# One input projection of a gated encoder block, moved from a two-stage product to a seven-product scheme done token-major beside the norm

## The chip, the core and the metric

The kernel runs on one core of a Trainium2 chip. A core has a matrix engine (TensorE, in the profile PE for its products and PEld for the loading of its stationary operands), a vector engine (VectorE, DVE), a scalar engine (ScalarE, ACT), a general engine (GpSimd, POOL) and a queue engine (SyncE, SP) that mostly issues transfers. Every engine works through its own instructions strictly in their order and waits where one of them needs something that is not there yet. Transfers that SP, ACT or POOL issue are moved by 16 DMA engines, which all of them share. On-chip memory is SBUF; PE writes into PSUM banks.

The metric is the time of one execution on the device in microseconds. Three runs of the kernel before gave a median of 924.56 us, from 924.12 to 924.88.

## What is computed

The reference is one layer of a gated encoder with 1024 tokens of width 1024. Cut to what matters here:

```python
h = rmsnorm(x, norm_g[l])
proj = h @ w_in[l]
q, k, v, za, u, vs, zs, gm = jnp.split(proj, IN_SPLITS, axis=-1)
...
sgo = chunked_spatial_gating(jax.nn.gelu(u, approximate=False),
                             jax.nn.gelu(vs, approximate=False),
                             sg_w[l], sg_b[l], sg_ln_g[l], sg_ln_b[l])
```

`chunked_spatial_gating` takes a layer norm over the 1024 channels of gelu(vs), and mixes blocks of 128 tokens. This case is about `vs` alone: a product of 1024 tokens by 1024 inputs by 1024 outputs, in single precision.

## The kernel before

Every product in this kernel is taken in three passes: an operand is split into a high part of the type fp32r (a cast on ACT) and the residual (a subtraction on DVE), and high by high, high by low and low by high are added in PSUM. One instruction multiplies a 128x128 stationary block with 512 columns. All products but that of `vs` use a seven-product scheme (Strassen's, in a form with four sums of weights and four sums of activations): both operands are cut into quarters, and seven quarter products stand in for eight. Its activation forms are called b11, t1, t2, b21, t3, b22 and t4 and lie in the slots `T_b11h`, `T_b11l` and so on (h is the high part, l the residual); `gemm_pair` walks through them (line 341 is its matmul).

`vs` comes first, and its layout is token-major: the tokens are the stationary operand, 512 output channels are the moving one. Here the eight products are all made, in two stages.

- **Stage 1, lines 599 to 621.** Tile t is 128 tokens, t from 0 to 7. `normed_tile` scales the rows of a tile (`scale_of`: a square with a sum on ACT, a few one-column instructions, then two multiplications of 512 columns at line 545), turns them with eight transposes on PE (line 551) and makes the high part (line 554, ACT) and the residual (line 555, DVE); a plain copy of each half goes to a raw slot (line 558, ACT). `vs_gemm` then takes the first 512 output channels of one tile: 8 blocks of inputs by 3 passes, 24 matmuls (line 596). Four weight tiles of 512 KB each are loaded into `T_t3h` and `T_t4h` (line 571) and split into `T_t1` and `T_t2` by `split_vs`. The program runs three tiles of the norm ahead of the products.
- **Stage 2, lines 680 to 705.** The last 512 output channels, for all eight tiles at once: eight PSUM banks, four weight tiles split through the rotating tiles `wh` and `wl` (line 156), and for each of them 8 tiles by 2 blocks by 3 passes (line 565). In between, `make_forms` builds t1, t2, t3 and t4 for the rest of the kernel from the raw slots, the gelu of the first half is taken (line 637), and `part_of_early` issues one transfer on POOL's queue after every second group (line 296): these add up weight sums of much later products in DRAM, and each of them waits for a matmul.
- Then the sums of rows of the mixing weights (line 712), a few small loads, and the first `gemm_pair`.

The instructions of each engine are put in an order of their own when the program is built, by a list scheduler that works on the program order and the tiles' dependencies; a load of the small constants can therefore stand between two loads of x. Tiles of one tag share a fixed number of buffers: x tiles and raw weight tiles share the three buffers of `wr`, so the load of x tile t can start once tile t-3 has been turned.

Two more facts of queues and buffers. A transfer that adds (`accum_op=ALU.add`) can only be issued by POOL, and POOL's queue is in order too. And the `junk` tile, into which line 531 writes the squares that nobody reads, is a `wl` buffer here, while the tile `wT` is only used for the mixing weights (loaded at line 681, cleared in part at line 682 on DVE).

Of the kernel before, what the change touches and what calls it, by code (L numbers as in the profile page):

```python
# [24 lines left out]
F32 = mybir.dt.float32  # L25
F32R = mybir.dt.float32r
# [4 lines left out]
P = 128  # L31
# [21 lines left out]
def hybrid_tile(  # L53
# [117 lines left out]
    def slot(name, shape=(P, 4, HALF), dt=F32R):  # L171

        return mtile(list(shape), dt, "T_" + name, 1)
# [317 lines left out]
    junk = mtile([P, D], F32, "wl", 3)  # L491
# [11 lines left out]
    g_in = [bank("o") for half in range(2)]  # L503
    for half in range(2):
# [4 lines left out]

    b12 = [  # L510
        [v[:].rearrange("p (a k c) -> p a k c", a=2, k=4)[:, i] for i in range(2)]
        for v in (mtile([P, D], F32R, "s", 2) for _ in range(2))
    ]
    b12 = [(hi, mtile([P, 4, P], F32R, "x", 5)[:]) for two in b12 for hi in two]
    f = {n: slot(at, dt=F32) for n, at in (("f11", "t3l"), ("f21", "t4l"))}
# [4 lines left out]
    def quarter_of(t, j):  # L520

        if t >= 4 and j == 0:
            return b12[t - 4]
        return [v[:, :, tokens(t)] for v in hb[("b11", "b21", "b22")[j if t < 4 else 2]]]

    casts = []

# [9 lines left out]
    def normed_tile(t, scale=None):  # L537
        xt, r = scale or scale_of(t)
        if t == 4:
            hb.update(new_b(("b22",)))  # L540
            f.update((n, slot(at, dt=F32)) for n, at in (("f12", "t4h"), ("f22", "t3h")))
        turned = []
        for j in range(2):
            cs = half_of(j)
            nc.vector.scalar_tensor_tensor(
                xt[:, cs], xt[:, cs], r[:], g_in[j][:], op0=ALU.mult, op1=ALU.mult
            )
            pt = bank("tp")
            for i in range(4):
                k = j * 4 + i  # L550
                nc.tensor.transpose(pt[:, i * P : (i + 1) * P], xt[:, k * P : (k + 1) * P], ident[:])
            p3 = pt[:].rearrange("p (k c) -> p k c", k=4)
            hi, lo = quarter_of(t, j)
            casts.append(nc.scalar.copy(hi, p3))
            nc.vector.tensor_sub(lo, p3, hi.bitcast(F32))
            turned.append((f[f"f{j + 1}{t // 4 + 1}"][:, :, tokens(t)], p3))
            if t:
                nc.scalar.copy(*turned.pop())
        return turned

    def vs_step(acc, t, k, wh, wl):

        hi, lo = (v[:, k % 4, :] for v in quarter_of(t, k // 4))
        for n, (lt, rt) in enumerate(((hi, wh), (hi, wl), (lo, wh))):
            mm = nc.tensor.matmul(acc, lt, rt, start=k == 0 and n == 0, stop=k == KC - 1 and n == 2)  # L565
        return mm

    vs_w = []

    def load_vs(c):  # L570
        nc.sync.dma_start(vs_raw[c // 2][:, c % 2, :], w[W_VS + c])

    def split_vs(c):

        raw = vs_raw[c // 2][:, c % 2, :].rearrange("p (k n) -> p k n", k=2)
        hi, lo = (v[c // 2][:, 2 * (c % 2) : 2 * (c % 2) + 2, :] for v in vs_split)
        if c:
            split(hi, lo, raw)
        else:

            for k in range(2):
                nc.scalar.copy(hi[:, k, :], raw[:, k, :])
                (nc.gpsimd if k else nc.vector).tensor_tensor(
                    lo[:, k, :], raw[:, k, :], hi[:, k, :].bitcast(F32), op=ALU.subtract
                )
        vs_w.extend((hi[:, k, :], lo[:, k, :]) for k in range(2))

    def vs_gemm(t):
        acc = bank("mm")
        for c in range(4):  # L590
            for n in range(3):
                for k in (2 * c, 2 * c + 1):
                    hi, lo = (v[:, k % 4, :] for v in quarter_of(t, k // 4))
                    wh, wl = vs_w[k]
                    lt, rt = ((hi, wh), (hi, wl), (lo, wh))[n]
                    nc.tensor.matmul(acc[:], lt, rt, start=k == 0 and n == 0, stop=k == KC - 1 and n == 2)  # L596
        nc.scalar.copy(xh[:, t, 0:HALF], acc[:])

    unsplit = normed_tile(0)
    keep_busy(0)  # L600
    vs_raw = [slot(n, (P, 2, D), F32) for n in ("t3h", "t4h")]
    vs_split = [[slot(n + e) for n in ("t1", "t2")] for e in "hl"]
# [8 lines left out]
    x_in[2] = load_x(2)  # L611
    for c in (2, 3):
        split_vs(c)
    for dst, src in unsplit:
        nc.scalar.copy(dst, src)
    normed_tile(1, second)
    normed_tile(2)
    for t in range(NT):
        vs_gemm(t)
        if t + 3 < NT:  # L620
            normed_tile(t + 3)


    def vs_weights(c):
        raw = raw_tile()
        nc.sync.dma_start(raw[:], w[W_VS + 4 + c])
        hi = mtile([P, D], F32R, "wh", 3)
        lo = mtile([P, D], F32R, "wl", 3)
        split(hi[:], lo[:], raw[:])
        return hi, lo  # L630
# [4 lines left out]
    def gelu_of(t):  # L635
        two = xh[:, t : t + 2, 0:HALF]
        after(nc.scalar.activation(two, two, AF.Gelu), casts[-1])
        for i in range(2):
            statistics(t + i, 0)

    def form(name, src, c):
        hi, lo = hb[name]
        cs = slice(c, c + 2)
        split(hi[:, cs, :], lo[:, cs, :], src, name == "t2")

    def make_forms():
        f11, f12, f21, f22 = (f[n] for n in ("f11", "f12", "f21", "f22"))
        hb.update(new_b(("t1",)))
        for c in range(0, 4, 2):
            cs = slice(c, c + 2)  # L650
            nc.vector.tensor_sub(f11[:, cs, :], f11[:, cs, :], f12[:, cs, :])
            form("t1", f11[:, cs, :], c)
            yield
        hb.update(new_b(("t2",)))
        for c in range(0, 4, 2):
            cs = slice(c, c + 2)
            nc.vector.tensor_add(f11[:, cs, :], f22[:, cs, :], f11[:, cs, :])
            form("t2", f11[:, cs, :], c)
            yield
        for c in range(0, 4, 2):  # L660
            cs = slice(c, c + 2)
            nc.vector.tensor_sub(f12[:, cs, :], f22[:, cs, :], f12[:, cs, :])
            yield
        last = []
        for c in range(0, 4, 2):
            cs = slice(c, c + 2)
            v = mtile([P, 2, HALF], F32, "s", 2)
            nc.vector.tensor_sub(v[:], f11[:, cs, :], f21[:, cs, :])
            last.append(v)
            yield  # L670
        hb.update(new_b(("t3",)))
        for c in range(0, 4, 2):
            form("t3", f12[:, c : c + 2, :], c)
            yield
        hb.update(new_b(("t4",)))
        for c in range(0, 4, 2):
            form("t4", last[c // 2][:], c)
            yield
# [6 lines left out]
    accs = [bank(tag) for tag in ("mm", "mm", "o", "o", "sc", "sc", "tp", "tp")]  # L685
    aside = [lambda t=t: gelu_of(t) for t in range(0, NT, 2)]
    forms = make_forms()
    aside[1:1] = [lambda: next(forms, None)] * 2
    aside += [lambda: next(forms, None)] * 11
    weights = [vs_weights(0), vs_weights(1)]  # L690
    for c in range(4):
        if c + 2 < 4:
            weights.append(vs_weights(c + 2))
        for t in range(NT):
            wh, wl = weights[c]
# [4 lines left out]
            if c == 3:  # L700
                nc.scalar.activation(xh[:, t, HALF:D], accs[t][:], AF.Gelu)
            if aside and t % 2:
                aside.pop(0)()
    while aside:
        aside.pop(0)()

    row_sums = [bank("sc") for half in range(2)]
    wh, wl = mtile([P, D], F32R, "wh", 3), mtile([P, D], F32R, "wl", 3)
    split(wh[:], wl[:], mix_w[:].rearrange("p g i -> p (g i)"))
    for half in range(2):  # L710
        for n, part in enumerate((wh, wl)):
            nc.tensor.matmul(row_sums[half][:], ones[:], part[:, half_of(half)], start=n == 0, stop=n == 1)
    of_head = sinks.rearrange("(c e r) -> e c r", e=2, r=2)
# [8 lines left out]
    for _ in range(3):  # L722
        split_next()
# [1022 lines left out]
```

## Time and profile before

| | us |
|---|---|
| median of three runs | 924.56 |
| lowest and highest | 924.12, 924.88 |
| span of the profiled execution | 921.3 |
| PE busy in that span | 904.7 |
| DVE busy | 691.5 |
| ACT busy | 521.8 |
| POOL busy | 126.8 |

The span runs from the first instruction of the program to the end of the last one; the time of a run is taken around the whole execution and is some 3.3 us longer (924.56 - 921.3). Three kinds of view are used below. The waits tell which engine stood still for whom. The timeline lists instructions with their start and duration, both in us. The windows give, for a stretch of time, the busy us of each engine with the number of its instructions in brackets, then the granted clock of PE (1.00 is full), the mean busy share of the DMA engines and the rate that they moved. Matmuls overlap, so the duration of one (0.39 us for 512 columns) is not its cost; the distance from one start to the next is.

### The profile page before, as it was taken

Reading aid. Unit: us, or ns where it says so; the run is one execution under the profiler, and the core shown is the slowest. Engines: PE = TensorE matmul, PEld = TensorE weight load, DVE = VectorE, ACT = ScalarE, POOL = GpSimd, SP = SyncE. Lnnn points to the kernel's source line nnn. Section 1 sums busy time; section 2 is a strip of 40 time slices with the busy share of each in tenths; the row PEclk is TensorE's granted clock in tenths of the full one; section 3 lists DMA queues with packets and bytes.
Section 4 is the critical chain, followed back from the end, with each engine's and each line's share of the span. In section 5 each row is a group of like instructions: output and inputs, shape, how many; then the busy total and the mean of one; then the engine's idle time right before and its main releaser. Section 6 shows DMA issues by size and latency. Waiting matters only on the chain.

```text
span 921.3 us, 13177 instructions
## 1 busy us (share of the span) xinstructions
PE 904.7 (98%) x4332; PEld 752.7 (82%) x4332; DVE 691.5 (75%) x1241; ACT 521.8 (57%) x1046; POOL 126.8 (14%) x188
## 2 busy tenths in 40 slices
PE   8999999999999999999999999999998999999996
PEld 5888888888888788888888888888877887878885
DVE  6875776656687668887778888747798589579996
ACT  6862443334444366767766766755665385367443
POOL 0002122213011001211101111101100111110012
PEclk9999999999999999999999999999999999999998
DMA  6427678877788676776786799689869755998632
GB/s 240 138 91 215 207 197 184 161 158 234 230 290 267 229 200 182 169 202 184 197 240 222 248 220 253 174 313 349 294 219 341 240 201 151 272 307 303 206 115 114
DMA packets 128734, 201.71 MB, mean 219 GB/s; under 512 B 12345, under 2 KB 60729, under 8 KB 128666
## 3 DMA queue, kind: packets, MB, share of 16 engines
q1 hardware_dynamic: 109512, 148.17, 48.8%
q0 software_dynamic: 19008, 52.44, 23.8%
q8 instruction: 34, 0.56, 0.3%
q14 instruction: 34, 0.28, 0.1%
q10 hardware_dynamic: 146, 0.27, 0.1%
HBM read 144.07 MB, written 86.11 MB: 250 GB/s over the span
## 4 chain that ended last, share of the span: by engine, by line
PE 85%; DVE 8%; DMA 4%; issue 2%; ACT 1%; SPq 1%; DVEq 0%; ACTq 0%
PE ps_mm L341 34%; PE ps_o L341 25%; PE ps_mm L596 5%; PE ps_sc L1076 3%; PE ps_o L1161 2%; PE ps_tp L341 2%; PE ps_tp L1120 2%; PE ps_sc L341 2%; PE ps_tp L764 2%; DVE wl L156 1%; PE ps_tp L565 1%; PE ps_sc L565 1%; PE ps_o L565 1%; PE ps_mm L565 1%; DVE bq L185 1%
## 5 line engine op out<-in xcount | busy, mean ns | idle before, releaser
L155 ACT CAST wh<-s 128x1024 fp32r<-128x1024 f32 (+1 forms) x78 | 78.1, 1005 | 87.2 <-PE ps_mm L341 49.9
L156 DVE TENSOR_TENSOR wl<-wr,wh 128x1024 fp32r<-128x1024 f32 (+1 forms) x80 | 75.7, 948 | 49.1 <-ACT wh L155 48.3
L155 ACT CAST wh<-wr 128x1024 fp32r<-128x1024 f32 (+1 forms) x80 | 66.3, 830 | 71.6 <-PE ps_mm L341 34.3
L156 DVE TENSOR_TENSOR wl<-s,wh 128x1024 fp32r<-128x1024 f32 (+1 forms) x78 | 90.9, 1166 | 9.3 <-ACT wh L155 9.2
L341 PE MATMUL ps_o<-T_t1h,wh 128*128 128x512 f32 x148 | 58.9, 398 | 0.8 <-ACT wh L155 0.7
L341 PE MATMUL ps_o<-T_b22h,wh 128*128 128x512 f32 x148 | 58.2, 394 | 0.0
L341 PE MATMUL ps_o<-T_t1h,wl 128*128 128x512 f32 x148 | 57.9, 391 | 0.3 <-DVE wl L156 0.3
L341 PE MATMUL ps_o<-T_b22l,wh 128*128 128x512 f32 x148 | 57.9, 391 | 0.0
L341 PE MATMUL ps_o<-T_b22h,wl 128*128 128x512 f32 x148 | 57.8, 390 | 0.0
L341 PE MATMUL ps_o<-T_t1l,wh 128*128 128x512 f32 x148 | 57.6, 390 | 0.0
L341 PE MATMUL ps_mm<-T_b11h,wl 128*128 128x512 f32 x140 | 54.8, 392 | 2.9 <-DVE wl L156 2.9
L341 PE MATMUL ps_mm<-T_t4h,wh 128*128 128x512 f32 x140 | 55.3, 395 | 0.5 <-DVE x L376 0.5
L341 PE MATMUL ps_mm<-T_t3l,wh 128*128 128x512 f32 x140 | 54.6, 390 | 0.6 <-DVE T_t3l L156 0.6
L341 PE MATMUL ps_mm<-T_t2h,wl 128*128 128x512 f32 x140 | 55.0, 393 | 0.0
L341 PE MATMUL ps_mm<-T_t2l,wh 128*128 128x512 f32 x140 | 55.0, 393 | 0.0
L341 PE MATMUL ps_mm<-T_b11h,wh 128*128 128x512 f32 x140 | 54.9, 392 | 0.0
L341 PE MATMUL ps_mm<-T_t3h,wh 128*128 128x512 f32 x140 | 54.9, 392 | 0.0
L341 PE MATMUL ps_mm<-T_t2h,wh 128*128 128x512 f32 x140 | 54.7, 391 | 0.0
L341 PE MATMUL ps_mm<-T_t4h,wl 128*128 128x512 f32 x140 | 54.7, 391 | 0.0
L341 PE MATMUL ps_mm<-T_t3h,wl 128*128 128x512 f32 x140 | 54.7, 390 | 0.0
L341 PE MATMUL ps_mm<-T_b11l,wh 128*128 128x512 f32 x140 | 54.6, 390 | 0.0
L1089 ACT ACTIVATE pr<-ps_sc,sm 128x192 f32<-128x192 f32 (+2 forms) x128 | 50.9, 410 | 6.5 <-DVE sm L1085 5.5
(356 smaller groups left out, 2399.6 us busy)
## 6 DMA issues: line engine op xcount, KB each, us to landing
wr<-in_w_dram SPq DMA_DIRECT2D x86, 256.0 KB
sums<-in_w_dram POOLq DMA_DIRECT2D x20, 512.0 KB, 5.6
s<-sums SPq DMA_DIRECT2D x20, 512.0 KB
q_hl<-qhl SPq DMA_DIRECT2D x16, 512.0 KB
q<-q_hl SPq DMA_DIRECT2D x64, 128.0 KB
wr<-in_w_dram SPq DMA_DIRECT2D x14, 512.0 KB
y_dr<-x POOLq DMA_DIRECT2D x28, 256.0 KB, 6.6
g<-in_w_dram POOLq DMA_DIRECT2D x12, 512.0 KB, 7.2
```

The costliest lines, as they stand in the source:

```text
L155: nc.scalar.copy(hi, src)
L156: return nc.vector.tensor_sub(lo, src, hi.bitcast(F32))
L185: op(dst[:, i : i + 2, :], a[:, i : i + 2, :], c[:, i : i + 2, :])
L341: nc.tensor.matmul(acc, lt, rt, start=fresh and k == 0 and n == 0, stop=k == 3 and n == 2, skip_group_check=True,)
L565: mm = nc.tensor.matmul(acc, lt, rt, start=k == 0 and n == 0, stop=k == KC - 1 and n == 2)
L596: nc.tensor.matmul(acc[:], lt, rt, start=k == 0 and n == 0, stop=k == KC - 1 and n == 2)
L764: nc.tensor.matmul(pm[:, t * P : (t + 1) * P], xh[:, half * 4 + t, g * P : (g + 1) * P], bias[-1][1][:, g % 4, :], start=True, stop=True,)
L1076: nc.tensor.matmul(sc[:, i, k0:], q_of[:, c, i * P : (i + 1) * P], kt[:, f, k0:], start=f == 0, stop=f == 1,)
L1089: nc.scalar.activation(held_in[c, i], sc[:, i, lo:hi], AF.Exp, bias=nmax[:, c, i : i + 1], scale=-1.0, accum_out=sums[:, c, i : i + 1],)
L1120: nc.tensor.transpose(dst, pr[:, i, block * P : block * P + width], ident[:])
L1161: nc.tensor.matmul(po[:, cs], lt, rt, start=n == 0, stop=n == len(terms) - 1)
```

## The change

`vs` is taken by the seven-product scheme too, token-major. With j the half of the tokens (tiles 0 to 3, and 4 to 7) and i the half of the output channels, four quarters of the result lie in `xh` as `x_place(i, j, t)`.

- For tiles 0 to 3 `first_tile` makes the forms b11 and b21, and `first_product` multiplies them by the weight quarters a11 and a12 (24 matmuls a tile, as before, but into two banks that are then added on ACT and DVE).
- For tiles 4 to 7 `second_tile` makes t1 and b22, on DVE from PSUM and from the copies that `first_tile` left in `xh`. Two adding transfers per tile (256 KB each, SBUF to SBUF) finish what t3 and t4 need.
- `by_s1` multiplies t1 by the weight sum s1 = a21 + a22, `by_s4` multiplies b22 by s4 = a12 + a11 + s1 (12 matmuls each a tile). `late_product` then takes t2 by s2 = a11 + s1, t3 by s3 = a21 + a11 and t4 by a22, 48 matmuls each, into the four banks that hold the b11 products.
- The weight sums are made by adding transfers on POOL's queue straight into the SBUF slots that hold the raw quarters: eight of 512 KB for s1, s4 and s2 and two more for s3, whose slot is loaded again (`load_part("s3", ...)`) once s1 has been read by all the others.
- `junk` is now in the buffer `wT`; x tiles 0 to 3 are turned through the banks `sc`, the gain stays in the banks `tp` until ACT copies it into `xh`.
- The stage of the forms (`make_forms`), and the four raw slots that it read, are gone.

The diff, cut to its core:

```diff
-    junk = mtile([P, D], F32, "wl", 3)
+    junk = mtile([P, D], F32, "wT", 1, pool)
+    nf12 = [xtile() for _ in range(4)]
...
+    def add_on(dst, src):
+        nc.gpsimd.dma_start(dst, src, accum_op=ALU.add)
...
+    def first_tile(t, scale=None):
+        xt, r = scale or scale_of(t)
+        left = []
+        for j, name in enumerate(("b11", "b21")):
+            pt = turned_half(xt, r, j)
+            form_of(name, t, by_k(pt[:]))
+            if j:
+                left.append(lambda pt=pt: nc.scalar.mul(raw_b21(t), pt[:], -1.0))
+            else:
+                left.append(lambda pt=pt: nc.scalar.copy(raw_sum(t), pt[:]))
+            if t:
+                left.pop()()
+        return left
+
+    def second_tile(t):
+        xt, r = scale_of(t)
+        if t == 4:
+            hb.update(new_b(("t1", "b22")))
+            f22.append(slot("t4l", dt=F32))
+        pt = turned_half(xt, r, 0)
+        nc.vector.tensor_sub(raw_sum(t), raw_sum(t), pt[:])
+        nc.scalar.mul(nf12[t - 4][:], pt[:], -1.0)
+        form_of("t1", t, by_k(raw_sum(t)))
+        pt = turned_half(xt, r, 1)
+        form_of("b22", t, by_k(pt[:]))
+        nc.scalar.copy(f22[0][:, t - 4, :], pt[:])
+        nc.vector.tensor_add(raw_sum(t), raw_sum(t), pt[:])
+        add_on(nf12[t - 4][:], f22[0][:, t - 4, :])
+        add_on(raw_b21(t), raw_sum(t))
...
+    def first_product(t):
+        accs[t] = bank("mm" if t < 2 else "tp")
+        vs_product(accs[t], "b11", t, "a11", True)
+        m2 = bank("o")
+        vs_product(m2, "b21", t, "a12", True)
+        nc.scalar.copy(x_place(0, 0, t), m2[:])
+        nc.vector.tensor_add(x_place(0, 0, t), x_place(0, 0, t), accs[t][:])
+
+    def by_s1(t):
+        t5s[t] = bank("o" if t < 2 else "sc")
+        vs_product(t5s[t], "t1", t, "s1", True)
+        nc.scalar.mul(x_place(1, 1, t), t5s[t][:], -1.0)
+
+    def by_s4(t):
+        vs_product(t5s[t], "b22", t, "s4", False)
...
     for c in (2, 3):
         load_vs(c)
     x_in[2] = load_x(2)
+    load_part("s1", "t4h", 1, 0)
     for c in (2, 3):
         split_vs(c)
...
+    for c in range(2):
+        add_on(flat(two_k(raws["s1"], c)), w_vs(1, 1, c))
+    for c in range(2):
+        add_on(flat(two_k(raws["a12"], c)), w_vs(0, 0, c))
+    for c in range(2):
+        add_on(flat(two_k(raws["a12"], c)), flat(two_k(raws["s1"], c)))
+    raws["s4"] = raws["a12"]
+    first_tile(1, second)
...
+    first_tile(2)
+    first_product(0)
+    first_tile(3)
+    first_product(1)
+    second_tile(4)
+    s1_hl = slot("t2h"), slot("t2l")
+    for c in range(2):
+        hi, lo = (two_k(v, c) for v in s1_hl)
+        split(hi, lo, two_k(raws["s1"], c))
...
+    first_product(2)
+    second_tile(5)
+    for c in range(2):
+        add_on(flat(two_k(raws["a11"], c)), flat(two_k(raws["s1"], c)))
+    raws["s2"] = raws["a11"]
+    first_product(3)
+    for c in range(2):
+        split_w("s4", c)
+    second_tile(6)
+    by_s1(0)
+    by_s1(1)
+    load_part("s3", "t4h", 1, 0)
+    for c in range(2):
+        add_on(flat(two_k(raws["s3"], c)), w_vs(0, 0, c))
+    second_tile(7)
+    by_s4(0)
+    by_s4(1)
+    a22 = []
+    for c in range(2):
+        a22.append(raw_tile())
+        nc.sync.dma_start(a22[c][:], w_vs(1, 1, c))
+    by_s1(2)
+    by_s1(3)
...
-    accs = [bank(tag) for tag in ("mm", "mm", "o", "o", "sc", "sc", "tp", "tp")]
...
-            for k in range(2):
-                ks = half_of(k)
-                pace[0] = vs_step(accs[t][:], t, 2 * c + k, wh[:, ks], wl[:, ks])
-            part_of_early()
...
+    late_product(
+        "t2",
+        "s2",
+        to_x12,
+        [lambda: split_w("s3", 0), make_t3]
+        + [lambda t=t: part_of("t3", t) for t in range(4)]
+        + [lambda: gelu_of(0), lambda: gelu_of(2)],
+    )
...
+    split_w("a22", 1, a22[1][:])
+    begin_job()
+    late_product("t4", "a22", to_x21, [split_next, lambda: gelu_of(4, 1), lambda: gelu_of(6, 1)])
```

More of the change, by code (lines that the diff above doesn't have):

```diff
@@ L501, in hybrid_tile @@
     keep_busy(2)
-    g_in = [bank("o") for half in range(2)]
+    g_in = [bank("tp") for half in range(2)]
     for half in range(2):
@@ L585, in split_vs, with vs_product @@
                 )
[L586 to L590, printed above, removed]
+        keep_w(name, c % 2, hi, lo)
+    def vs_product(acc, name, t, weight, fresh, last=True, cs=(0, 1)):
+        bh, bl = hb[name]
+        for c in cs:
             for n in range(3):
                 for k in (2 * c, 2 * c + 1):
[L593 to L597, printed above, removed]
@@ L603, in hybrid_tile, with keep_t5 @@
+    def by_s4(t):
+        vs_product(t5s[t], "b22", t, "s4", False)
+    def keep_t5(t):
+        nc.scalar.copy(x_place(0, 1, t), t5s[t][:])
+    unsplit = first_tile(0)
+    for name, at in (("a11", "t3h"), ("a12", "t3l")):
+        raws[name] = slot(at, dt=F32)
     load_vs(0)
@@ L611, in hybrid_tile @@
     x_in[2] = load_x(2)
+    load_part("s1", "t4h", 1, 0)
     for c in (2, 3):
         split_vs(c)
[L614 to L630, printed above, removed]
+    for move in unsplit:
+        move()
@@ new lines, in hybrid_tile @@
+    for c in range(2):
[6 more added lines that the diff above has]
+    first_tile(1, second)
+    g_sb = xh[:, 6:8, HALF:D]
+    for half in range(2):
+        after(nc.scalar.copy(g_sb[:, half, :], g_in[half][:]), casts[-1])
+    g_of[:] = [g_sb[:, half, :] for half in range(2)]
@@ L632, in statistics @@
+    for t in range(4):
+        form_of("t2", t, by_k(raw_sum(t)), True)
+    by_s4(2)
+    by_s4(3)
+    split_w("s2", 1)
+    for t in range(4):
+        keep_t5(t)
     def statistics(t, half):
         nc.vector.bn_stats(stats[:, t, half, :], xh[:, t, half_of(half)])
[L635 to L678, printed above, removed]
@@ L680, in hybrid_tile, with gelu_of @@
+    def gelu_of(t, half=0):
+        two = xh[:, t : t + 2, half_of(half)]
+        after(nc.scalar.activation(two, two, AF.Gelu), last_cast)
+        if half == 0:
+            for i in range(2):
+                statistics(t + i, 0)
     mix_w = mtile([P, KC, P], F32, "wT", 1, pool)
@@ L721, in hybrid_tile @@
     nc.sync.dma_start(lb_sb[:], ln_b)
-    for _ in range(3):
+    for _ in range(2):
         split_next()
```

175 lines of the change are left out of this document (111 added, 64 removed).

## The prediction

> **What bounds the kernel now.** I read the page's busy shares and its chain first, then what PE waited for in the stretch of the change, then the windows of that stretch.
>
> ```profile
> span 921.3 us, 13177 instructions
> ...
> PE 904.7 (98%) x4332; PEld 752.7 (82%) x4332; DVE 691.5 (75%) x1241; ACT 521.8 (57%) x1046; POOL 126.8 (14%) x188
> ...
> PE 85%; DVE 8%; DMA 4%; issue 2%; ACT 1%; SPq 1%; DVEq 0%; ACTq 0%
> ```
>
> ```profile
> PE ps_sc L498 <- DVE T_b22l L494: 1.9, 1, 1.9
> PE ps_tp L551 <- issue: 0.5, 1, 0.5
> ```
>
> ```profile
> 0.00:10.00 10.00, 7.57 (x17) 3.91 (x17) 4.63 (x11) 5.58 (x9) 2.13 (x8) 1.00 0.81 282
> 10.00:20.00 10.00, 9.85 (x41) 7.32 (x41) 7.90 (x19) 8.47 (x16) 0.00 (x0) 1.00 0.64 221
> 20.00:30.00 10.00, 10.00 (x52) 7.91 (x52) 8.08 (x24) 8.16 (x18) 0.00 (x0) 1.00 0.46 155
> ...
> 50.00:60.00 10.00, 10.00 (x46) 8.29 (x45) 6.99 (x10) 4.42 (x6) 0.00 (x0) 1.00 0.15 52
> ```
>
> PE is the bound, of the whole and of this stretch: the two rows of waits are all that it waited for in the first 260 us. In stage 1 ACT and DVE are 80% busy and PE still never waits. So a matmul that is dropped is worth its pitch, as long as PE is fed as densely as now; and DMA engines that are half idle are what the new adding transfers will use. The pitch is read from the end of stage 2:
>
> ```profile
> 97.72 0.39 PE L565 MATMUL ps_o<-wl,T_b21h 128*128 128x512 f32 x1
> ...
> 105.43 0.39 PE L565 MATMUL ps_tp<-wh,T_b22l 128*128 128x512 f32 x1
> 105.66 0.39 PE L712 MATMUL ps_sc<-wh,ones 128*128 128x512 f32 x1
> ...
> 106.59 0.39 PE L341 MATMUL ps_mm<-T_b11h,wh 128*128 128x512 f32 x1
> ```
>
> 35 matmuls stand from 97.72 to 105.43, so the pitch is 7.71 / 34 = 0.227 us. The first `gemm_pair` starts at 106.59; all behind it is the same in both kernels, so what this start moves, the end moves.
>
> **The gain.** Before: 8 tiles by 2 halves by 24 matmuls, 384. After: 24 for tiles 0 to 3, and 12 each for s1, s4, s2, s3 and a22 over four tiles, 4 x (24 + 60) = 336. 48 x 0.227 = **10.9 us** off the path if nothing new stops PE.
>
> **The price of an adding transfer.** The trace has none into SBUF. The nearest are 512 KB adds into DRAM: the last three of the group below, issued one behind the other, ran alone in 540 to 546.
>
> ```profile
> L442 POOL DMA_DIRECT2D g<-in_w_dram x12: 515/536/1424, 459.9 to 537.7; - x12
> ...
> DMA to landing us min/median/max: 3.6/7.0/13.3
> ```
>
> ```profile
> 4.00:12.00 8.00, 7.48 (x18) 4.29 (x19) 5.50 (x13) 5.90 (x11) 1.40 (x1) 1.00 1.00 365
> 540.00:546.00 6.00, 6.00 (x35) 5.15 (x35) 5.20 (x13) 3.33 (x11) 0.82 (x1) 1.00 1.04 191
> ```
>
> Both windows have all 16 engines busy; loads move 365 GB/s, adds 191. So 524 kB cost 1.44 us of the engines as a load and 2.74 as an add. For an add into SBUF I take 2.74: the share of 1.04 says that the engines themselves were full, not that DRAM was awaited. Its bounds are 1.44 (as a load) and 3.7 (the slowest landed after 13.3, third in its row; less 2.3, which a load takes beyond its engine time, below: 11.0 / 3). The Trainium skill, "Collectives: The Full Stack", section "The bandwidth ceiling: the fold count and why AG ≠ RS ≠ AR", says that an add in a transfer is slow since it needs two source reads through one ring, wherever they lie; half of 365 is 183 GB/s, an estimate of 2.87 us per add, and with it the sum below would come out about 1 us later. The trace's 191 agrees, and no run here shows the SBUF side yet.
>
> **First stall: the first half of s1.** As the changed kernel is built, PE makes tiles 0 and 1 as before, and comes to tile 2 where it does now:
>
> ```profile
> 12.80 1.23 DVE L156 TENSOR_TENSOR T_t2l<-T_t4h,T_t2h 128x1024 fp32r<-128x1024 f32 x1 [0.79 <-ACT T_t2h L155]
> ...
> 14.46 1.22 DVE L156 TENSOR_TENSOR T_t2l<-T_t4h,T_t2h 128x1024 fp32r<-128x1024 f32 x1
> ...
> 18.04 0.33 SPq L487 DMA_DIRECT2D wr<-in_x_dram  x1
> ...
> 23.00 8.73 SPq L487 DMA_DIRECT2D wr<-in_x_dram  x3
> ...
> 24.39 0.41 PEld L596 LDWEIGHTS ps_mm<-T_t1h,T_b11h 128*128 128x128 f32 x2
> ```
>
> In ACT's queue the cast of s1's first half stands right before the b11 cast of tile 2, which tile 2's product needs, so ACT, and PE behind it, wait for the landing of that sum. On POOL's queue the sum is third: the two adds of a11 onto a12 come first, and wait until a12 has been split, 14.0 and 15.7 (ends of the first two rows). So it is issued at about 16.2 (0.5 us an issue). When does it land? By 10.0 the engines have moved 2.82 MB, 5.4 loads; nine are due now (x0 to x2, a11, a12, and the new a21), the last at 10 + 3.6 x 1.44 = 15.2. Beside the adds come x3, x4 (18.04), x5 (23.00) and a bias of half the size, 3.5 x 1.44 = 5.0; three adds are 8.2. Shared engines give 15.2 + 5.0 + 8.2 = 28.4, and about 1 until the semaphore: **29.5**.
>
> ```profile
> L155 ACT CAST wh<-wr 128x1024 fp32r<-128x1024 f32 x5 | 5.3, 1059 | 8.4 <-PE ps_tp L565 7.9 <-DMA wr<-in_w_dram 0.5
> ...
> L554 ACT CAST T_b11h<-ps_tp 128x512 fp32r<-128x512 f32 x4 | 2.4, 588 | 1.9 <-PE ps_tp L551 1.9
> ```
>
> With 1.06 and 0.59 for the two casts PE goes on at 31.1: it stood 31.1 - 24.4 = **6.7 us**. The residual of that b11 is behind s1's residual on DVE, another **0.4**.
>
> **Second stall: x tile 6.** The slot of a21 is loaded again for s3, and this load waits for all adds that read s1. SP's queue is in order, and behind it stand the loads of x6 and x7. s1's second half lands at 29.5 + 2.74 = 32.2; four adds (two onto a12, two onto a11) wait for the halves and run behind it, 11.0 more: 43.2. Then half of a21 and x6:
>
> ```profile
> 0.74 0.39 SPq L487 DMA_DIRECT2D wr<-in_x_dram  x1
> ...
> 4.43 1.06 ACT L531 ACTIVATE wl<-wr 128x1024 f32<-128x1024 f32 x1 [1.64 <-DMA wr<-in_x_dram]
> ```
>
> A load takes 4.43 - 0.74 = 3.7 to arrive; x6 is there at 43.2 + 0.4 + 1.44 + 3.7 = 48.7. On ACT its square (1.06) stands before the copy of the s1 product of tile 0 (0.59), and s4 of tile 0 may not add into that bank before the copy: 50.4. PE had 60 matmuls and 16 transposes from 31.5, 13.6 + 2.1 (half a tile's four take 0.52, below), so it is through at 47.2: **3.2 us**.
>
> ```profile
> 26.34 0.55 PEld L551 LDWEIGHTS ps_tp<-ident,wr 128*128 128x128 f32 x4
> ...
> 26.86 0.30 PEld L596 LDWEIGHTS ps_mm<-T_t1h,T_b11h 128*128 128x128 f32 x2
> ```
>
> **Third stall: the mixing weights.** Their load is now behind the last square, since `junk` took their buffer; before, it went out at 10.60 and was covered.
>
> ```profile
> 10.60 0.43 SPq L681 DMA_DIRECT2D wT<-in_sg_w_dram  x1
> ...
> 19.72 0.48 DVE L682 MEMSET wT<- 64x512 f32 x1 [0.16 <-DMA sink_sb<-in_sinks_dram]
> ```
>
> x7 comes two loads behind x6 with an add of s3 between, 48.7 + 2.9 + 2.7 = 54.3; its square ends at 55.4, and the load arrives at 59.1 alone or 61.8 with one add ahead of it. I take 61. On DVE the memset stands before the residuals of tile 6 and the scaling of tile 7: 0.48, then three of 0.69, some small ones and the scaling:
>
> ```profile
> L545 DVE SCALAR_TENSOR_TENSOR wr<-wr,st,ps_o 128x512 f32<-128x512 f32 x16 | 11.2, 745 | 0.2
> ...
> L555 DVE TENSOR_TENSOR T_b11l<-ps_tp,T_b11h 128x512 fp32r<-128x512 f32 x4 | 2.8, 690 | 2.5 <-ACT T_b11h L554 2.5
> ```
>
> So tile 7 is turned at about 64.4. PE has 36 matmuls and 16 transposes from 50.4 and is there at 60.7: **3.7 us**. The casts of tile 7 that the next product waits for add about **0.9**.
>
> **The clock.** Behind a wait of 1.4 us PE's granted clock was halved once in this trace:
>
> ```profile
> PE ps_sc L1076 <- ACT pr L1089: 1.4, 1, 1.4
> ```
>
> ```profile
> 325.50:329.00 3.50, 3.50 (x12) 2.71 (x11) 2.13 (x9) 2.97 (x14) 0.00 (x0) 0.51 0.90 207
> ```
>
> 3.5 us at half rate lose 1.7. Behind stalls 1 and 2 the next stall, set by transfers, absorbs that; behind the third nothing does: **1.7**.
>
> **What costs nothing.** The last part (t2, t3, t4) is 144 matmuls, 32.7 us of PE, over six splits of weights (1.06 ACT, 1.22 DVE), twelve forms (0.59, 0.69), some eight sums (0.69) and the statistics, about 25 us of DVE and 20 of ACT; without that cover each split would cost 2.3. Fifteen paced transfers stand where sixteen did. The loads of the first `gemm_pair` go out some 20 us later, still over 30 us ahead of use.
>
> **Sum.** 6.7 + 0.4 + 3.2 + 3.7 + 0.9 + 1.7 = 16.6, less 10.9: +5.7. The profiled execution is 921.3 and some 3.3 around it, 924.6, which is the median of the runs too. Forecast: **930.3 us**.
>
> **Rivals.**
> - *Adds into SBUF run like loads* (1.44). s1 lands at about 15.2 + 5.0 + 4.3 + 1 = 25.5, PE stands 2.7; the chain for x6 ends ten microseconds earlier, before PE needs it, and mixing weights too. 2.7, the small 0.4 and 0.9, and the clock's 1.7, now not absorbed, are 5.7 against 10.9: 924.6 - 5.2, **919.4**. For it: the sum is neither read from DRAM nor written to it. Against it: the full engines in 540 to 546. It wins from an add under 2.1 us on.
> - *Adds into SBUF are slower still* (3.7). Eight stand on the way to x6: 8 x 0.96 = 7.7 more, **938**. For it: 13.3 us, and loads of x in between; against it: the median of that group is 7.0.
> - *The clock stays low longer*: each of the three stalls followed by two half windows, 3.4 where 1.7 is counted and 1.5 of stall 2 not absorbed, **933.5**. The Trainium skill, "TensorE: Matmul & The Clock Gate", section "Part 1: The HAM clock gate", has the gate close after a window of about 3.4 us without work; by that rule stalls 1 and 3 alone would bring it, and the row above, after 1.4, goes further.
> - *The casts don't hold PE*: if s1's split came late enough, all 10.9 stay: **913.7**. Against it: the built order of ACT's queue.
>
> **How the numbers follow.** Forecast 0.57, adds like loads 0.15, slower adds 0.12, clock 0.11, no stall 0.05. 0.2% (1.8 us) is about what runs of this kernel tell from no change. Faster: 0.15 + 0.05 = 0.20; within: 0.05, from the near end of the forecast's own range (926 to 935); slower 0.75. The range holds all but the last rival: 919 to 939.
>
> **What would show it.** Right: PE idle some 6 us from about 24 with ACT waiting for a transfer into `T_t4h`, again near 47 behind x6 and near 61 behind DVE's memset of `wT`; s1's halves landing near 30; the first L341 at about 112. Wrong: an add of 512 KB into SBUF that lands within 4 us in a row of three, PE dense from 24 to 50, and an L341 before 106.

## The result, and the profile after

| | median us | runs, from to | ratio to the kernel before |
|---|---|---|---|
| before, beside it | 924.3 | 4, 922.8 to 924.9 | |
| changed | 938.7 | 4, 937.8 to 941.2 | 1.0166, 95% interval 1.0147 to 1.0185 |
| changed, run again (e5 below) | 941.2 | 5, 938.0 to 944.1 | 1.0184, 1.0165 to 1.0203 |

The change costs 14 to 17 us where 5.7 were forecast. The profiled execution of the changed kernel was the slowest of its four: 941.2 us for a span of 939.4, 2.5 above the median. Runs that list both have 1.8 us between span and time, so the profiled 921.3 us of before belong to a run about 1 us faster than the median. Of the 18.1 us between the two spans 3.5 are therefore such differences.

The page of the changed kernel, busy shares and chain:

```profile
span 939.4 us, 13191 instructions
...
PE 904.0 (96%) x4284; PEld 749.5 (80%) x4284; DVE 697.7 (74%) x1263; ACT 528.3 (56%) x1060; POOL 142.9 (15%) x206
...
PE 80%; DVE 8%; DMA 7%; issue 2%; ACT 1%; SPq 0%; DVEq 0%; ACTq 0%
```

PE makes 48 matmuls less and is busy just as long (904.0 us; before 904.7): some of them took longer. DMA holds 7% of the chain instead of 4%. What PE waited for, over the whole span (us in all, times, longest):

```profile
PE ps_tp L650 <- ACT T_b11h L557: 5.0, 1, 5.0
PE ps_sc L548 <- DVE wr L544: 4.3, 1, 4.3
PE ps_mm L341 <- DVE wl L156: 2.9, 2, 1.7
PE ps_mm L341 <- ACT x L366: 2.3, 1, 2.3
PE ps_o L650 <- ACT xh L674: 2.1, 2, 1.8
...
PE ps_tp L650 <- DVE T_b11l L558: 1.7, 1, 1.7
PE ps_sc L650 <- ACT x L581: 1.2, 1, 1.2
PE ps_tp L880 <- DVE xh L858: 1.1, 2, 0.8
PE ps_tp L880 <- DVE x L896: 0.9, 1, 0.9
```

The three stalls of the prediction are there: tile 2 (5.0 and 1.7), the bank behind x6's square (1.8), tile 7 (4.3 and 1.2). The 2.9 is in both kernels. The rows of L366, L858 and L896 are new, and they lie behind the start of the first `gemm_pair`, where nothing was forecast: a fourth stall. The timeline says what held ACT and DVE (start, duration, then the idle time before it and what ended it):

```profile
28.15 1.04 ACT L155 CAST T_t2h<-T_t4h 128x1024 fp32r<-128x1024 f32 x1 [6.56 <-DMA T_t4h<-in_w_dram]
29.10 0.58 ACT L557 CAST T_b11h<-ps_sc 128x512 fp32r<-128x512 f32 x1
...
31.55 0.20 DVE L834 TENSOR_SCALAR nsink_sb<-sink_sb 128x8 f32<-128x8 f32 x1 [9.77 <-DMA sink_sb<-in_sinks_dram]
...
51.15 1.06 ACT L536 ACTIVATE wT<-wr 128x1024 f32<-128x1024 f32 x1 [2.08 <-DMA wr<-in_x_dram]
...
64.83 0.48 DVE L768 MEMSET wT<- 64x512 f32 x1 [5.15 <-DMA wT<-in_sg_w_dram]
...
118.30 0.39 PE L341 MATMUL ps_mm<-T_b11h,wh 128*128 128x512 f32 x1
...
125.98 0.69 DVE L242 TENSOR_TENSOR s<-wr 128x512 f32<-128x512 f32 x1 [6.95 <-DMA wr<-in_w_dram]
```

Each wait in brackets ends with a transfer. Two were not in the prediction: `nsink` (L834), a negation of eight numbers per partition that stands on DVE ahead of tile 2's residuals and waits 9.8 us for a 2 KB transfer, and the weight sums of the second job (L242), 7.0 us. The first L341 starts at 118.30; before it was 106.59, so 11.7 us are lost ahead of it and 6.4 behind. Stretches of the span (length, busy us and count of PE, PEld, DVE, ACT, POOL, then granted clock, DMA share, GB/s):

```profile
24.90:28.35 3.45, 0.00 (x0) 0.00 (x0) 0.00 (x0) 0.20 (x1) 0.00 (x0) 1.00 1.00 176
28.35:38.58 10.23, 7.12 (x16) 5.14 (x17) 6.15 (x13) 5.58 (x10) 3.46 (x4) 0.50 1.04 239
38.58:41.00 2.42, 2.42 (x17) 2.04 (x16) 0.80 (x3) 1.33 (x4) 0.00 (x0) 1.00 1.09 217
62.90:65.89 2.99, 0.36 (x2) 0.00 (x0) 1.03 (x2) 0.00 (x0) 0.00 (x0) 1.00 1.07 296
65.89:76.13 10.24, 7.35 (x21) 5.68 (x22) 6.77 (x13) 5.01 (x7) 3.45 (x4) 0.50 0.81 164
...
100.00:110.00 10.00, 10.00 (x46) 8.26 (x45) 8.20 (x11) 5.07 (x5) 2.75 (x4) 1.00 0.98 247
110.00:120.00 10.00, 10.00 (x46) 8.29 (x45) 8.21 (x21) 4.35 (x6) 2.64 (x5) 1.00 0.95 262
```

Behind the first and the third stall the clock is halved for 10.2 us each time, not for 3.4; a start every 0.43 us instead of 0.227 costs some 3.2 and 3.5 us there (an estimate from the starts in these stretches). And the DMA engines are full again from 100 to 120 us, where the sums in DRAM run.

### The profile page after: what moved, and what is told of

It reads as the page before. It is cut to its first block, busy times and chain, and to the rows that moved or that the text cites. A ratio compares the mean times of both kernels' runs of the same rounds, so it can differ in the third digit from the quotient of the medians.

```text
span 939.4 us, 13191 instructions
## 1 busy us (share of the span) xinstructions
PE 904.0 (96%) x4284; PEld 749.5 (80%) x4284; DVE 697.7 (74%) x1263; ACT 528.3 (56%) x1060; POOL 142.9 (15%) x206
## 3 DMA queue, kind: packets, MB, share of 16 engines
q0 software_dynamic: 21600, 59.78, 28.1%
## 4 chain that ended last, share of the span: by engine, by line
PE 80%; DVE 8%; DMA 7%; issue 2%; ACT 1%; SPq 0%; DVEq 0%; ACTq 0%
PE ps_mm L341 35%; PE ps_o L341 25%; PE ps_sc L1192 3%; DMA wr<-in_w_dram 3%; PE ps_tp L341 3%; PE ps_o L1277 2%; PE ps_sc L341 2%; PE ps_tp L1236 2%; PE ps_sc L650 1%; DVE wl L156 1%; DMA sink_sb<-in_sinks_dram 1%; PE ps_tp L650 1%; PE ps_tp L880 1%; PE ps_mm L650 1%; DMA wT<-in_sg_w_dram 1%
## 5 line engine op out<-in xcount | busy, mean ns | idle before, releaser
L156 DVE TENSOR_TENSOR wl<-wr,wh 128x1024 fp32r<-128x1024 f32 (+1 forms) x78 | 73.3, 942 | 45.5 <-ACT wh L155 43.8
L155 ACT CAST wh<-wr 128x1024 fp32r<-128x1024 f32 (+1 forms) x78 | 64.1, 824 | 63.0 <-PE ps_mm L341 30.4
L341 PE MATMUL ps_o<-T_t1h,wh 128*128 128x512 f32 x148 | 58.8, 397 | 0.8 <-ACT wh L155 0.7
L341 PE MATMUL ps_o<-T_b22h,wh 128*128 128x512 f32 x148 | 58.2, 393 | 0.0
L341 PE MATMUL ps_mm<-T_b11h,wl 128*128 128x512 f32 x140 | 55.2, 394 | 2.9 <-DVE wl L156 2.9
L341 PE MATMUL ps_o<-T_b22l,wh 128*128 128x512 f32 x148 | 57.8, 391 | 0.0
L341 PE MATMUL ps_o<-T_b22h,wl 128*128 128x512 f32 x148 | 57.8, 390 | 0.0
L341 PE MATMUL ps_o<-T_t1h,wl 128*128 128x512 f32 x148 | 57.7, 390 | 0.0
L341 PE MATMUL ps_o<-T_t1l,wh 128*128 128x512 f32 x148 | 57.6, 389 | 0.0
L341 PE MATMUL ps_mm<-T_t3h,wh 128*128 128x512 f32 x140 | 55.1, 393 | 2.3 <-ACT x L366 2.3
L341 PE MATMUL ps_mm<-T_t4h,wh 128*128 128x512 f32 x140 | 55.4, 396 | 0.6 <-DVE x L376 0.6
L341 PE MATMUL ps_mm<-T_b11h,wh 128*128 128x512 f32 x140 | 55.4, 396 | 0.0
L341 PE MATMUL ps_mm<-T_t3l,wh 128*128 128x512 f32 x140 | 54.6, 390 | 0.6 <-DVE T_t3l L156 0.6
L341 PE MATMUL ps_mm<-T_t2l,wh 128*128 128x512 f32 x140 | 55.2, 394 | 0.0
L341 PE MATMUL ps_mm<-T_b11l,wh 128*128 128x512 f32 x140 | 55.1, 394 | 0.0
L341 PE MATMUL ps_mm<-T_t2h,wl 128*128 128x512 f32 x140 | 55.0, 393 | 0.0
L341 PE MATMUL ps_mm<-T_t2h,wh 128*128 128x512 f32 x140 | 55.0, 393 | 0.0
L341 PE MATMUL ps_mm<-T_t4h,wl 128*128 128x512 f32 x140 | 54.8, 392 | 0.0
L341 PE MATMUL ps_mm<-T_t4l,wh 128*128 128x512 f32 x140 | 54.8, 391 | 0.0
```

The costliest lines, as they stand in the source:

```text
L155: nc.scalar.copy(hi, src)
L156: return nc.vector.tensor_sub(lo, src, hi.bitcast(F32))
L341: nc.tensor.matmul(acc, lt, rt, start=fresh and k == 0 and n == 0, stop=k == 3 and n == 2, skip_group_check=True,)
```

## The experiments

Ratios below are to the kernel before, run on the same chip in the same batch.

**e1: without the adding transfers.**

```diff
-    for c in range(2):
-        add_on(flat(two_k(raws["s1"], c)), w_vs(1, 1, c))
...
-        add_on(flat(two_k(raws["s3"], c)), w_vs(0, 0, c))
```

> The ten adding transfers that make s1, s2, s3 and s4 are left out, so the plain parts stand in their places and the output is not the reference's. Theory (transfer chain): everything up to the turning of tile 7 (67.6 us in the changed kernel) waits in the end for the DMA engines, which the adds keep full. Then the three stalls (7.0 + 2.0 + 5.9 us) and both stretches at half clock (3.2 + 3.5) go: first L341 at 118.3 - 21.6 = about 97, time 938.7 - 21.6 = about 917, unless the late stall behind the first L341 grows. Rival (the order of the casts and the missing buffer are to blame, not the adds): the waits at x6 and the mixing weights stay, time over 930.

919.1 us, ratio 0.9941 (0.9925 to 0.9958), first L341 at 98.1. PE's waits from 12 to 100 us are these two rows; no half-rate stretch is left before 300 us:

```profile
PE ps_sc L650 <- ACT x L581: 0.9, 1, 0.9
PE ps_sc L548 <- issue: 0.2, 1, 0.2
```

So without the adds there is no loss ahead of the first L341, and the 48 matmuls are worth what was said: 8.4 us earlier, plus these 1.1 and another 1.3 in gaps too short for the list of waits, make 10.8. The late waits (L366, L858, L896: 1.6 + 1.1 + 0.9) stay; they have another cause.

**e5 and e6: the changed kernel again, and the price of an add.** e6 issues the same ten transfers for the weight sums, which overwrite; those of tiles 4 to 7 still add:

```diff
-    def add_on(dst, src):
-        nc.gpsimd.dma_start(dst, src, accum_op=ALU.add)
+    def add_on(dst, src, op=ALU.bypass):
+        nc.gpsimd.dma_start(dst, src, accum_op=op)
```

> The changed kernel once more, unaltered, on the chip of the next three runs, as their base. 937.5 to 939.5, and first L341 between 115 and 119: the profiled execution so far was the slowest of four (941.2 against a median of 938.7), so that its stalls are the upper end.

> The ten transfers that make the weight sums are issued where and when they were, with the same waits and bytes, but overwrite instead of adding, so the output is not the reference's. Theory (price of an add): each then takes 1.4 us of the 16 engines where it took 2.7, 13 us less in all before tile 7; s1's halves land near 24, x6 and the mixing weights land about 10 us earlier, the second and third stall and both half-rate stretches go: 921 to 926. Rival (it is the chain of waits from transfer to transfer, not the engines' time): 932 or more.

e5: 941.2 us, first L341 at 117.6. e6: 929.8 us, ratio 1.0056 (1.0041 to 1.0070), first L341 at 106.9. In this order of the queues the adding alone costs 11.5 us of e5's loss, near the 13 of engine time. The 921 to 926 forecast for e6 failed, for the first stall and 6.8 us at half rate stayed, and x6's square and the mixing weights came 4 and 8 us earlier than in e5 (46.3 and 56.4 against 50.0 and 64.1), not 10. Of the second stall 0.9 us were left in both; the third and the half rate behind it went, as expected. Issues from 14 to 33 us, with the median from issue to landing (changed kernel first, then e6 from 14 to 36):

```profile
T_t4h<-in_w_dram POOLq DMA_DIRECT2D x2, 512.0 KB, 12.6
T_t3l<-T_t4h POOLq DMA_DIRECT2D x2, 512.0 KB, 9.7
T_t3h<-T_t4h POOLq DMA_DIRECT2D x2, 512.0 KB, 11.7
```

```profile
T_t4h<-in_w_dram POOLq DMA_DIRECT2D x2, 512.0 KB, 8.0
T_t3l<-T_t4h POOLq DMA_DIRECT2D x2, 512.0 KB, 8.3
T_t3h<-T_t4h POOLq DMA_DIRECT2D x2, 512.0 KB, 9.0
```

The last four of these, from SBUF to SBUF, landed 2.5 us apart as adds and 1.24 us apart as copies. The first stall stayed, although s1's first half is there at 23.7, as forecast, and ACT casts at once. Now DVE stands (timeline of e6):

```profile
29.19 0.17 DVE L834 TENSOR_SCALAR nsink_sb<-sink_sb 128x8 f32<-128x8 f32 x1 [7.29 <-DMA sink_sb<-in_sinks_dram]
```

PE waits 4.7 us for the residual behind it: the first stall has two locks.

**e11: one of the two locks alone.**

```diff
-    nc.vector.tensor_scalar_mul(nsink_sb[:], sink_sb[:], -1.0)
+    after(nc.vector.tensor_scalar_mul(nsink_sb[:], sink_sb[:], -1.0), last_split)
```

> Only DVE's nsink is ordered behind the last split, all else as in the changed kernel. Theory (first stall has two locks, ACT's cast of s1 and DVE's nsink, and x6's load sets what follows anyway): PE's second wait at tile 2 gets about 1.5 us shorter, x6 lands as before, time within 1.5 us of the changed kernel's. Rival (each stall has its own price): 2 us or more saved.

941.5 us, ratio 1.0194 (1.0173 to 1.0215), first L341 at 117.7 (e5: 117.6). Waits of PE up to 100 us, e5 and then e11:

```profile
PE ps_tp L650 <- DVE T_b11l L558: 4.0, 1, 4.0
PE ps_tp L650 <- ACT T_b11h L557: 2.4, 1, 2.4
...
PE ps_o L650 <- ACT xh L674: 0.9, 2, 0.7
```

```profile
PE ps_o L651 <- ACT xh L675: 7.1, 2, 6.8
...
PE ps_tp L651 <- ACT T_b11h L557: 1.9, 1, 1.9
```

PE waits 4.5 us less at tile 2 (I expected 1.5) and 6.1 us longer for the bank behind x6's square. What follows is set by x6's landing: the 4.5 us taken off the first stall bought nothing.

**e2: the memset later.**

```diff
-    nc.vector.memset(mix_w[64:128, :, 0:64], 0.0)
+    after(nc.vector.memset(mix_w[64:128, :, 0:64], 0.0), mix_after)
```

`mix_after` is the residual of s2's second half.

> DVE's memset of wT, which waits for the mixing weights, is ordered behind the residual of s2's second half. Theory: the third stall (4.5 + 1.4) and the half-rate stretch behind it (3.5) hang on this one wait, so that tile 7 is turned at about 63 and the first L341 comes at 109 to 111: 929 to 931. Rival (the wait only passes to the next transfer in the chain, the adds of tiles 5 to 7): less than 3 us saved, 936 or more.

932.9 us, ratio 1.0091 (1.0073 to 1.0108), first L341 at 109.6, as expected; the time is 2 us above the forecast, and the two medians of the changed kernel, 938.7 and 941.2, differ by as much. PE stands 1.3 us for the next in the chain where it stood 5.5, and no half-rate stretch follows. Unlike the first stall this one had nothing behind it to take the gain back.

**e3: the third stall filled with work.**

```diff
+                if (weight, t, c, n) == ("s4", 1, 1, 2):
+                    after(turns[7], hold(acc, 18))
```

`hold` issues matmuls with zeros into the same bank; `turns[7]` is the first transpose of tile 7.

> 18 more matmuls with a stationary operand of zeros stand where PE waits for tile 7 (4.1 us of work in a stall of 4.5); nothing else is changed. Theory (the granted clock falls because PE stands still): the half-rate stretch from 65.9 is gone, PE's pitch after the stall is 0.227, and 3.5 us are saved: 935.2. Rival (the clock falls for another cause): the stretch stays and the time is 938.7 or a little more.

938.4 us, ratio 1.0153 (1.0137 to 1.0169): the time is the rival's, not the 935.2 of the theory, and can't be told from the changed kernel's. The windows settle the cause of the clock, where 62 to 66 is the filled stall:

```profile
62.00:66.00 4.00, 4.00 (x19) 3.25 (x18) 0.99 (x2) 0.00 (x0) 0.00 (x0) 1.00 1.10 282
66.00:70.00 4.00, 2.94 (x16) 1.87 (x15) 3.52 (x8) 0.82 (x2) 1.74 (x2) 1.00 0.86 166
70.00:76.00 6.00, 5.28 (x23) 4.24 (x23) 3.67 (x6) 5.62 (x8) 1.72 (x2) 1.00 1.06 221
```

The clock stays at 1.00 from 62 to 76, so behind this stall it was PE's standing still that halved it. The first L341 comes at 115.5, which is 2.8 and 2.1 us earlier than in the two profiles of the changed kernel, where 3.5 were expected; these two differ by 0.7 themselves.

**e4: the sums in DRAM spread.**

```diff
     def by_s4(t):
-        vs_product(t5s[t], "b22", t, "s4", False)
+        pace[0] = vs_product(t5s[t], "b22", t, "s4", False)
+        if t > 1:
+            part_of_early(1)
...
-                if t % 3:
-                    part_of_early(1)
-                elif c:
-                    part_of_early()
+                part_of_early()
```

(and the same in `by_s1`).

> The paced sums in DRAM are spread: four are issued beside the last s1 and s4 products and then one with every second half-product, where ten of fifteen stood 1.36 us apart. Theory (fourth stall: DVE waits 6.9 us for the second job's weights because sums fill the DMA engines in 100 to 128): this wait falls below 2 us, the waits of PE behind the first L341 (2.3 + 1.1 + 0.9) go, and the first L341 stays near 118: 934.4 to 936. Rival (that load is late because its buffer comes free late, at 113.7): unchanged, 938.7.

934.5 us, ratio 1.0105 (1.0079 to 1.0130), first L341 at 116.9. DVE's longest wait for the second job's weights falls to 2.7 us (I expected under 2), and PE waits for nothing from 105 to 250 us. From issue to landing a sum takes 6.0 us (median of the page) where it took 8.5, and 5.6 before. The fourth stall is thus the paced sums' density: fifteen in 31 us instead of sixteen in 41.

**e7 to e10: all waits moved, the transfers kept.** e7 has the edits of e2, e4 and e11, and `second_tile(7)`, with x7's load, ahead of the loads that bring a21 again for s3. e8 adds the order of the splits: s1's casts and residuals behind the forms of tile 5, s4's behind tile 6, two `keep_t5` later. e9 puts them behind the scalings of tiles 6 and 7 too. e10 lets adds wait:

```diff
+        add_on(flat(two_k(raws["a12"], c)), w_vs(0, 0, c), squares[3])
...
+        add_on(flat(two_k(raws["a11"], c)), flat(two_k(raws["s1"], c)), squares[6])
```

> Four of the waits are moved out of the way and the casts of s1 are left where they are: nsink behind the last split, the memset of wT behind s2's second half, x7's load ahead of the second load of a21, the paced sums spread. Theory: the first stall and the half rate behind it stay (7 + 3), the rest goes except 1 to 2 us; -2.0 - 5.9 - 3.5 - 4.3 + 2 = -13.7 from the changed kernel: 925 to 928. Rival (each wait that goes is replaced by the next transfer of the same chain): 931 or more.

> As the run before, and the casts and residuals of s1 stand behind the forms of tile 5, those of s4 behind tile 6, and two copies of t5 behind t3's second form. The same transfers, adds and matmuls in another order. Theory (all stalls are queue order; the adds themselves can be covered): of the 10.9 us gained some 4 are lost to waits of 1 to 1.5 us at tiles 6 and 7 and at t3's second half, and up to 2 to the clock: before - 5, 918 to 921, first L341 at 100 to 103. Rival (the DMA engines are full to 70 us, and no order hides 27 us of adds): 924 or more.

> As the run before it (all waits moved), but the split of s1 stands behind the forms of tile 5 and the scaling of tile 6, that of s4 behind the forms of tile 6 and the scaling of tile 7, since there the scaling of tile 6 stood behind the residuals of s1 and PE waited 2.0 us for it at 54. Theory (queue order is what is left): two of the 7 us that PE waits there go, 920 to 922 against 923.0. Rival (the late squares of tiles 3 to 5, whose loads landed 8 to 12 us after issue, are what is left, and the order of the splits is no matter): 922.5 to 924.

> As the one before, and the adding transfers give way to the loads of x: s1's two go first, those of a11 and s1 onto a12 wait for the square of tile 3, those of s1 onto a11 for the square of tile 6. Theory (x tiles 3 and 4 landed 8 and 11 us after issue because four to six adds shared the engines with them): the squares of tiles 3 and 4 come 2 to 4 us earlier, PE waits less than 3 us up to tile 7, 917 to 920. Rival (the same bytes have to go before s4 is needed, the wait only moves behind tile 7): the time of the run before, within 1.5 us.

| | median us | ratio, 95% interval | first L341 |
|---|---|---|---|
| e7 | 925.2 | 1.0010, 1.0000 to 1.0020 | 108.1 |
| e8 | 923.0 | 0.9982, 0.9969 to 0.9996 | 106.2 |
| e9 | 923.9 | 0.9997, 0.9984 to 1.0010 | 105.5 |
| e10 | 923.8 | 0.9998, 0.9988 to 1.0008 | 104.2 |

e7 came as expected: of the whole loss the first stall (4.5 us) with 6.8 us at half rate is left, and three waits of about 1 us. e8 came between its theory (918 to 921) and its rival (924): the first stall is gone, but PE waits as long for the scaling of later tiles, now behind x's own loads. Still, e8 has every add of e5, and 18 us of e5's time are gone by order alone. The longest waits of PE in e8:

```profile
PE ps_sc L558 <- DVE wr L554: 5.4, 2, 3.6
PE ps_sc L558 <- ACT T_t4l L603: 1.6, 1, 1.6
```

Its x4 was squared at 26.9 and x5 at 35.0, 8.6 and 12.2 us after their issue (the expectations of e9 and e10 call them tiles 3 and 4); a load takes 3.7 when alone. e9 and e10 followed their rivals. In e10 the wait for the scaling fell to 2.4 us and no half-rate stretch was left before 700 us, but the waits behind the first `gemm_pair` were back.

**e12 and e13: fewer transfers in the stretch.** e12 is e10 without paced sums before the first `gemm_pair`; e13 also makes the eight adds of tiles 4 to 7 on DVE:

```diff
+    for t in range(4):
+        nc.vector.tensor_add(raw_b21(t), raw_b21(t), raw_sum(t))
+    for t in range(4):
+        nc.vector.tensor_add(nf12[t][:], nf12[t][:], f22[0][:, t, :])
```

> As e10, but none of the paced sums in DRAM is issued before the first gemm_pair; they follow it, and the fifteen that are then behind are made up for in the last stage. Theory (engine time): the DMA share falls from 80 us on, the weights of the second job land earlier, the waits of PE at the first gemm_pair and behind it (1.8 + 1.1 + 0.9) go: 919 to 921. Rival (queue order, or the sums are missed later): 923 or more.

> As e12, and the eight adding transfers of tiles 4 to 7 (256 KB each, 11 us of the engines at the measured price) are eight sums on DVE (0.69 us each), behind the forms of t2, where DVE is a third busy. Theory (engine time): what stands behind them (s3, a22, the first job's loads) comes earlier, first L341 at 100 to 103, 1 to 3 us below e12: 916 to 919. Rival (DVE becomes what PE waits for, or these transfers were off the path): the time of e12 or more.

e12: 922.3 us, ratio 0.9976 (0.9963 to 0.9989); e13: 924.5, 1.0004 (0.9990 to 1.0018). Stretches of e12:

```profile
32.00:48.00 16.00, 10.69 (x43) 7.62 (x42) 9.83 (x24) 10.10 (x19) 6.90 (x8) 0.89 1.02 219
48.00:64.00 16.00, 14.35 (x66) 11.27 (x67) 15.05 (x25) 12.11 (x19) 2.58 (x3) 1.00 1.06 292
64.00:80.00 16.00, 16.00 (x73) 13.23 (x72) 9.06 (x14) 10.49 (x17) 2.64 (x3) 1.00 0.50 95
80.00:96.00 16.00, 16.00 (x72) 13.25 (x71) 14.19 (x22) 8.65 (x11) 0.00 (x0) 1.00 0.09 34
```

From 64 us on PE is dense and the waits behind the first L341 are gone, as the engine-time theory has it, but the time stayed above its 919 to 921. e13 followed its rival: the first L341 came at 108.4, not at 100 to 103, and taking the x adds off the DMA engines bought nothing. Most of what is left stands in 32 to 48: PE is busy 10.7 of 16 us, the DMA engines are full, and PE waited 5.0 us for the scaling of one x tile. With the same code up to there that wait was 1.8 us in e10's profile, so single profiles do not rank these kernels. Whether another order of adds and loads in 16 to 50 us would save those 5 us was not tried. By their intervals e12 and e8 are faster than the kernel before, by 0.24% (0.11 to 0.37) and 0.18% (0.04 to 0.31); e7, e9, e10 and e13 can't be told from it.

## Why the prediction was wrong in size

The sign and the three stalls were right, and their makers in the main; the sum was 8.7 us short (5.7 forecast, 14.4 measured). Step by step, by the profiled execution:

| step | forecast | measured |
|---|---|---|
| gain of 48 matmuls | 10.9 | 10.8 (e1) |
| 512 KB add, SBUF to SBUF | 2.74 | 2.5 between landings |
| first stall | 6.7 + 0.4 | 5.0 + 1.7 |
| x6's square starts | 48.7 | 51.15 |
| second stall | 3.2 | 1.8 |
| x7's square starts | 54.3 | 54.06 |
| mixing weights, from issue to the memset | 5.6 | 9.4 |
| tile 7's turning | 64.4 | 67.6 |
| wait for its casts | 0.9 | 1.2 |
| half rate behind the third stall | 1.7 | 3.5 |
| late part and behind | 0 | 4.3 of waits, 1.7 of clock |

- *The price of an add* was right, and in this order of the queues it is worth 11.5 us (e6); that order can hide most of it is what e8 shows. The Trainium skill's two source reads, cited in the prediction from "Collectives: The Full Stack", section "The bandwidth ceiling: the fold count and why AG ≠ RS ≠ AR", agree also for SBUF: 2.5 us as an add is twice the 1.24 of the copy. That section speaks of reductions between cores; that it reaches to SBUF is what the landings here show. The rival "adds like loads" is refuted by the landings. Its 919.4 is not borne out either: e6, where only the adds of tiles 4 to 7 still add, is at 929.8.
- *First stall*: the size was right, half the reason was not. That the residual adds only 0.4 behind s1's was wrong: in the profile quoted above it stood behind `nsink` until 32.8, in e5 PE waited longer for that than for ACT. In the trace of before, the row of 19.72 has DVE waiting 0.16 us for the same transfer, and I took its lateness for nothing. The "about 1 until the semaphore" in this step is a term that no run shows by itself; s1's first half landed at 28.1, where 29.5 was forecast.
- *"The loss behind stalls 1 and 2 is absorbed"* was right (e11 shows such absorbing: 4.5 us less at tile 2, 6.1 more at x6). x6 came 2.4 us late: the adds were through at 44.6, 1.4 after the 43.2 of the forecast, and from there to x6's square it took 6.5 us, not 5.5. But this went no further, since x7's square started at 54.06, where 54.3 was forecast.
- *Third stall*: the mechanism was right (e2 takes it away by one order on DVE), the load of the mixing weights was mis-sized. It went out at 55.43, as forecast, and was taken to need 5.6 us, with at most one add ahead of it. Three adds, s3's second half and the two of tile 4, and a load of a22 (55.00) had been issued ahead of it and were still under way (timeline, then size and us from issue to landing of the adds):

```profile
52.68 0.86 POOL L531 DMA_DIRECT2D T_t4h<-in_w_dram  x1 [2.77 <-DMA T_t4h<-in_w_dram]
53.22 1.22 POOL L531 DMA_DIRECT2D x<-T_t4l  x1
53.75 1.57 POOL L531 DMA_DIRECT2D xh<-xh  x1
54.06 1.06 ACT L536 ACTIVATE wT<-wr 128x1024 f32<-128x1024 f32 x1 [1.18 <-DMA wr<-in_x_dram]
55.43 0.87 SPq L767 DMA_DIRECT2D wT<-in_sg_w_dram  x1
```

```profile
T_t4h<-in_w_dram POOLq DMA_DIRECT2D x1, 512.0 KB, 6.5
x<-T_t4l POOLq DMA_DIRECT2D x1, 256.0 KB, 8.2
xh<-xh POOLq DMA_DIRECT2D x1, 256.0 KB, 10.3
```

The adds landed at 59.2, 61.4 and 64.0, and DVE's memset started at 64.83, 9.4 us after the load's issue (9.5 in e5; 4.7 in e6). That made tile 7's turning 3.2 us later than forecast.
- *The clock*: the forecast took the one stretch of before, 3.4 us, as the size of all. The two here are three times that. The Trainium skill, "TensorE: Matmul & The Clock Gate", section "Part 1: The HAM clock gate", says that the gate judges in free-running windows of 3413 ns and opens after a busy one; the stretches of 10.24 and 3.41 us are whole multiples of it, and they agree: after 28.35 the first two windows each held a part of the stall, only the third was dense. My rival "the clock stays low longer" had this loss nearly right, 3.4 us behind the third stall; I gave it 0.11.
- *"What costs nothing"* is the step that failed outright. Fifteen paced transfers "stand where sixteen did" only by count; in a shorter stretch they filled the engines (0.95 to 0.98 from 100 to 120 us, above). And I looked at the loads of the first job alone; loads of the second job went out at 113.7, behind sums that took 8.5 us each, and DVE needed them at 119. e4 takes back the 4.3 us of PE.

Added up, the first L341 was forecast at 112.3 and came at 118.3: 3.2 from the load of the mixing weights, 0.3 from tile 7's casts, 1.8 from the clock, and 0.7 in small waits. Behind it come 4.3 of the fourth stall, 0.4 of small ones, and 1.7 of a half-rate stretch of 3.4 us at 717.8. The profile of before does not have that stretch, but nor has e5's of the same changed kernel, so it is not shown to be the change's. Together this is more than the 8.7, because the profiled executions are not the medians (3.5 us, above).

## What to carry to other kernels

An adding transfer into SBUF took twice the DMA time of a copy here (2.5 against 1.24 us for 512 KB), so "free" sums in transfers must be paid from idle engine time at that place; add up the bytes of the whole stretch, paced background transfers and the next stage's loads among them. When such a chain is late, ask for each engine what else stands in its queue behind a transfer, however small: a negation of eight numbers held PE as long as a weight matrix did. And removing one stall of a chain pays only if nothing later waits for the same transfers: here 4.5 us less in the first of three bought nothing, and the last, taken away, brought the first L341 forward by some 8 us (e2).

## What the runs showed that was not expected

- A 2 KB transfer into `sink_sb`, issued at 18.4, was waited for until 31.55, and until 29.19 in e6, where s1's 512 KB, issued at 16.6, were there at 23.7. In e1, without the ten big transfers beside it, the wait for it was over at 23.14. So it is the company of the big transfers, not its size, that made it late.
- Half-rate stretches behind stalls of some 5 us were 10.2 us in the changed kernel, 6.8 behind the first stall of e2, e4, e6 and e7, and 3.4 in e8, e9 and e12: all whole multiples of 3.41 us.
